# Two fused transformer blocks on one core: the fifth and sixth weight slot run side by side in the start-up, and three smaller edits

## The chip, the cores and the metric

The kernel runs on one core of a Trainium2 chip. The metric is the device time of one execution in microseconds, as a median of runs. An engine works through its own queue in order: TensorE (PE) multiplies matrices, its weight loads are shown as PEld, VectorE is DVE, ScalarE is ACT, SP issues most of the transfers.

## What is computed

Two blocks of two layers each act on x of 512 tokens by 1024 features, batch 1, in fp32. The first block's layer is a modulated RMS norm, an input projection to 28 column tiles of 128, three token mixers (a 31-tap convolution, dilated window attention, and HGRN2, a gated linear scan in both directions), an output projection, and a convolutional FFN. The second block's layer has a top-k sparse attention (A), a sliding-window attention with sinks (B) and stick-breaking attention (C). The two parts that the change touches most, cut:

```python
# modulation and norm, ahead of the input projection
mod = cond @ w_ada[l] + b_ada[l]
sh1, sc1, g1, sh2, sc2, g2 = split(mod, 6)
h = rmsnorm(x, norm1_w[l]) * (1 + sc1) + sh1        # then h @ w_in

# stick-breaking: A[t,s] = beta_ts * prod_{s<j<t}(1 - beta_tj), s < t
z = einsum('bthd,bshd->bhts', qb, k) * dh ** -0.5
log_beta = log_sigmoid(z)
log_1m = where(strict, log_sigmoid(-z), 0.0)
after = cumsum(log_1m, reverse=True) - log_1m
a = where(strict, exp(log_beta + after), 0.0)
```

## The kernel before

Features lie on the 128 partitions, tokens along the free axis. Weights come in *slots*: one slot is one tile of 128 output columns, 8 chunks of 128x128 that multiply the 8 tiles of h (128x512). A product with fp32 accuracy is made of three products of rounded parts: with w = hi + lo and h = hh + hl it is hi·hh, hi·hl, lo·hh (`k_step`, line 811). `w_hi` (746) makes hi with a copy that `copy` (367) gives to ScalarE or VectorE, whichever its clocks say is done first; `w_lo` (764) makes lo = raw - hi on VectorE. `his`, `splits` and `loads` (787, 793, 778) bring the slots up to a number to the state copied, split, loaded. The raw weights have three buffers, so a load waits until the lo of the slot three before is made.

The order of all instructions on each engine is the program's. A planner writes it: streams (attention, scan, convolution) are generators, and `run` (820) and `products` (849) step them between the projection's matmuls whenever the planner's own clocks say that their operands are there. `Timed.charge` keeps these clocks by a cost for each operation.

`start_up` (542) has an order written out by hand. The modulation is a product with `w_ada`, done on VectorE: one row of 128 outputs is one load of 512 KB (`ada`) and one scalar_tensor_tensor with an accumulator over 128x1024 (`mac`). The eight scale rows come first. The first FIRST = 4 slots (`duo`) don't wait for the norm: they multiply x times its scale in plain fp32, tile by tile, as x and the scale rows land (`prep`, `h_raw`); the norm's factor per token (`self.rb`) multiplies their sums afterwards (`scaled`), and the shift's part comes in as a bias, `bias_mm` (961): for each of the eight tiles, one-column products of the four slots' weights with the shift column, eight records of TensorE. The eight shift rows are loaded and multiplied next (`shift`, 593), each a row of 128x1024 and an addition of one column. Then h itself is made for the slots after the fourth: `h_tile` (1148) makes t = x·A1·rb on VectorE, hh = t + B on ScalarE (rounded), and hl = (t + B) - hh on VectorE.

In the kernel before all eight shift rows stand ahead of or among the first two h tiles (lines 612 to 632), all eight bias tiles stand on TensorE ahead of the fifth slot, the splits of slots five to seven are set among the h tiles by WAT, and slot five runs only when `start_up` is over, in `run`, then slot six. `norm_done` adds the bias to the four sums and spawns `hand_on` (997), which gives them to their consumers. `lower_bounds` (692), a dozen small operations and one Exp for the scan's gates, is made during the last start-up tile.

`attend` (1184) serves all attentions: for a tile of 128 queries it makes the scores of two heads on TensorE in a PSUM bank, `score` turns them into weights, `rest` finishes these, then they are transposed and multiplied with V. In `attC_stream` (1894) `score` takes two sigmoids of the scores, of -z and of z; a strict triangular mask is added to the scores on TensorE as a product of a bf16 identity with a bf16 mask (lines 1216 to 1219, `extra`); `rest` scans the first from the right with products and multiplies. `att1_stream` (1326) is the window attention; its `rest` normalises one head on VectorE and one on ScalarE. `scan_stream` (1361) has seven levels; in each, two products of 128x256 update the keys K of both directions (1406 to 1409).

Of the kernel before, what the change touches and what calls it, by code (L numbers as in the profile page):

```python
# [17 lines left out]
P = 128  # L18
S = 512
# [20 lines left out]
RAWAT = (5, 7)  # L40
WAT = [0, 1, 2, 6, 7, 9]
# [153 lines left out]
class Kernel:  # L195
# [297 lines left out]
    def setup(self):  # L493
# [12 lines left out]
        self.hraw = {}  # L506
        self.held_done = 0
# [17 lines left out]
        self.strb = ct("strb", [P, P], BF16)  # L525
        self.idb = ct("idb", [P, P], BF16)
# [15 lines left out]
    def start_up(self):  # L542
# [3 lines left out]
        duo = self.slots[:FIRST]  # L546
# [25 lines left out]
        for n in range(KT):  # L572
            ada(n)
            self.load(self.x[:, n, :], self.i["xT"][:, n, :])
            if n in (0, 2, 3):
                c = slice(*((0, 2 * P), None, (2 * P, 4 * P), (4 * P, KT * P))[n])
                for d in duo:
                    self.load(d.raw[:, c], d.src[:, c])
# [19 lines left out]
        for n in range(KT):  # L598
            if n < KT - 1:
                prep(n + 1)  # L600
            else:
# [7 lines left out]
                lower = self.lower_bounds()  # L609
                next(lower)  # L610
                self.act(self.warm, self.ones[:, 0:1], AF.Sqrt)
                shift(0)
                next(lower, None)
                shift(1)
            for j, (d, p) in enumerate(zip(duo, accs)):
# [26 lines left out]
        self.splits(FIRST + 3)  # L642
        for t in tmps:
            t.free()
# [3 lines left out]
        self.norm_done(duo, ts, bb, True)  # L648

# [25 lines left out]
    def load_consts(self):  # L675
# [12 lines left out]
        self.acopy(self.strb, self.strf)  # L688
        self.acopy(self.idb, self.ident)
# [56 lines left out]
    def w_hi(self, j):  # L746
# [14 lines left out]
        self.copy(s.hi[:, :n], s.raw[:, :n])  # L761
# [422 lines left out]
    def attend(self, heads, span, stride, size, score, V, vo, tag, done, extra=0, groups=((0,), (1,), (2,), (3,))):  # L1184

# [9 lines left out]
        for g in range(len(groups) + 1):  # L1195
            new = []
            for qt in groups[g] if g < len(groups) else ():
                kt0, n = span(qt)
                small = n <= 256
                Ps, tmp = [], []  # L1200
                for bufs, units in ((Ps, 1 if small else 2), (tmp, extra // 2 if small else extra)):
                    for _ in range(units):
                        bufs.append((yield from self.alloc(1)))
                m, x = ([b.ap[:, o:o + n] for b in bufs for o in range(0, U, 256 if small else U)] for bufs in (Ps, tmp))
                new.append((qt, kt0, n, m, x, Ps, tmp))
            if new:
                scs = yield from self.banks("sc")
                at, views = 0, []
                for qt, kt0, n, *_ in new:
                    views.append([sc[:, at:at + n] for sc in scs])  # L1210
                    for hh in range(2):
                        rows = slice(64 * hh, 64 * hh + 64)
                        self.mm(views[-1][hh], q.ap[rows, qt * P:(qt + 1) * P], k.ap[rows, kt0 * P:kt0 * P + n],
                                not (extra and at), not extra, 0.858 * n / S)
# [5 lines left out]
                for (qt, kt0, n, m, x, Ps, tmp), sc in zip(new, views):  # L1220
                    self.did = 0.0
                    rest = score(qt, n, sc, m, *x)
                    made.append((qt, kt0, n // P, m, Ps, tmp, rest, self.did - 0.2))
# [3 lines left out]
            for _ in groups[g - 1] if g else ():  # L1227
                j, kt0, nk, m, Ps, tmp, rest, t = made.pop(0)
# [4 lines left out]
                for x in tmp:  # L1233
                    x.free()
# [91 lines left out]
    def att1_stream(self, p, q, k, vbox, out):  # L1326
# [12 lines left out]
        def score(qt, n, sc, m):  # L1339
# [21 lines left out]
    def scan_stream(self, l, p, q, T0b, Kb, vbox, gbox, out):  # L1361
# [37 lines left out]
        for lev in range(7):  # L1399
# [494 lines left out]
    def attC_stream(self, q, k, vbox, gbox, ys, key, tag):  # L1894
# [15 lines left out]

        def done():
# [3 lines left out]
                                    tag, done, 2, CAUSAL)  # L1915
# [436 lines left out]
```

## Time and profile before

| | |
|---|---|
| median of three runs | 2576.47 us (2575.38 to 2577.38) |
| profiled execution | 2577.97 us |
| its span | 2576.1 us |
| TensorE busy | 98% of the span |
| VectorE busy | 69% |
| ScalarE busy | 52% |
| granted clock, mean | 0.996 |

The profile is one execution. A line of the timeline has the start, the length in us, the engine, the line of the program (L114 and L348 are helpers through which all go, so the tiles' names tell operations apart), the operation, output<-input, shapes, a count where equal instructions are merged, and in brackets how long the engine stood idle before it and what ended that. Matmuls overlap their neighbours, so their pace is read from starts, not from lengths. [...]

### The profile page before, as it was taken

The page shows a single profiled execution, that of the slowest core. Times are in us where ns is not written, and L with a number is a line of the kernel's source. Part 1 is how long each engine was busy: PE and PEld are TensorE (multiplying, and loading weights), DVE is VectorE, ACT ScalarE, POOL GpSimd, SP SyncE. Part 2 cuts the span into 40 slices and gives each one's busy share as a digit, 9 for nine tenths or more (in the row PEclk, how much of TensorE's full clock was granted, in tenths as well). Part 3 has the DMA queues.
Part 4 walks back from the last instruction along what each step waited for, and adds up shares of the span by engine and source line. Part 5 has one row for each costly group of instructions (what it writes and reads, how often), then busy time and mean ns, then how long its engine had stood idle before and what let it go on. Part 6 is the DMA issues. An engine that isn't in the chain of part 4 may idle for free.

```text
span 2576.1 us, 39146 instructions
## 1 busy us (share of the span) xinstructions
PE 2520.9 (98%) x15404; PEld 1991.2 (77%) x15404; DVE 1771.2 (69%) x3364; ACT 1338.2 (52%) x2343; POOL 0.2 (0%) x4
## 2 busy tenths in 40 slices
PE   9999999999999999999999999999999999999998
PEld 5767788888976768888887667777789667777787
DVE  7897777656679768665667985566556895546645
ACT  4686653323357665442336455667435556656622
POOL 0000000000000000000000000000000000000000
PEclk9999999999999999999999999999999999999999
DMA  6433324444333222444342223232332112222222
GB/s 255 140 133 127 123 98 145 147 150 153 116 121 123 98 92 90 139 139 139 131 139 83 75 74 107 93 108 100 110 126 95 66 62 86 91 78 91 86 91 90
DMA packets 90071, 290.32 MB, mean 113 GB/s; under 512 B 10016, under 2 KB 13728, under 8 KB 89888
## 3 DMA queue, kind: packets, MB, share of 16 engines
q1 hardware_dynamic: 87728, 281.76, 32.5%
q10 hardware_dynamic: 2160, 6.06, 0.7%
q8 instruction: 122, 2.00, 0.3%
q14 instruction: 61, 0.50, 0.1%
HBM read 285.69 MB, written 2.10 MB: 112 GB/s over the span
## 4 chain that ended last, share of the span: by engine, by line
PE 77%; DVE 14%; ACT 6%; issue 2%; DMA 2%; SPq 0%; ACTq 0%; DVEq 0%
PE proj L348 65%; DVE arena L114 7%; PE sc L348 6%; ACT arena L114 3%; PE tr L352 3%; PE pva L348 2%; DVE lo L114 2%; DVE sm L114 2%; ACT L114 1%; PE pvs L348 1%; DVE stay L114 1%; PE tr L348 1%; DVE hl L114 1%; DVE ada L114 1%; ACT hi L114 0%
## 5 line engine op out<-in xcount | busy, mean ns | idle before, releaser
L348 PE MATMUL proj<-hh,hi 128*128 128x512 f32 (+1 forms) x2232 | 894.8, 401 | 7.8 <-ACT arena L114 2.7
L348 PE MATMUL proj<-hl,hi 128*128 128x512 f32 (+1 forms) x2232 | 869.1, 389 | 5.9 <-DVE hl L114 5.7
L348 PE MATMUL proj<-hh,lo 128*128 128x512 f32 (+1 forms) x2232 | 869.4, 390 | 0.5 <-DVE lo L114 0.5
L348 PEld LDWEIGHTS proj<-hh,hi 128*128 128x128 f32 x2232 | 420.0, 188 | 133.0 <-issue 36.9
L114 DVE TENSOR_TENSOR lo<-raw,hi 128x1024 fp32r<-128x1024 f32 (+2 forms) x381 | 436.1, 1145 | 94.9 <-ACT hi L114 90.7
L348 PEld LDWEIGHTS proj<-hh,lo 128*128 128x128 f32 x2232 | 419.8, 188 | 90.3 <-DVE lo L114 1.0
L348 PEld LDWEIGHTS proj<-hl,hi 128*128 128x128 f32 x2232 | 420.5, 188 | 86.8 <-DVE hl L114 9.1
L114 ACT CAST hi<-raw 128x1024 fp32r<-128x1024 f32 (+2 forms) x343 | 336.2, 981 | 98.7 <-PE proj L348 63.6
L348 PE MATMUL proj<-rar,hi 128*128 128x512 f32 x672 | 208.8, 392 | 0.0
L114 DVE SCALAR_TENSOR_TENSOR arena<-proj,colt,arena 128x511 f32<-128x511 f32 x164 | 122.9, 749 | 103.8 <-ACT arena L114 100.9
L114 DVE TENSOR_TENSOR arena<-arena 128x512 f32<-128x512 f32 (+10 forms) x316 | 169.7, 557 | 24.6 <-ACT arena L114 17.8
L114 ACT ACT_TABLE_LOAD x132 | 169.4, 1283 | 18.3 <-DVE sm L114 5.7
L114 ACT COPY arena<-tr 128x512 f32<-128x512 f32 (+3 forms) x259 | 109.0, 459 | 119.3 <-PE tr L352 110.1
L114 DVE SCALAR_TENSOR_TENSOR ada<-ada,cbc 128x1024 f32<-128x1024 f32 x128 | 155.8, 1218 | 0.2 <-DMA ada<-ada 0.2
L114 ACT ACTIVATE arena<-proj 128x512 f32<-128x512 f32 x121 | 71.6, 599 | 154.8 <-PE proj L348 152.0
L348 PEld LDWEIGHTS proj<-rar,hi 128*128 128x128 f32 x672 | 124.8, 188 | 28.3 <-issue 3.3
L114 ACT ACTIVATE arena<-proj,colt 128x512 f32<-128x512 f32 x82 | 56.4, 687 | 171.1 <-PE proj L348 169.0
L114 ACT ACTIVATE arena<-arena,sm 128x512 f32<-128x512 f32 (+3 forms) x195 | 114.2, 586 | 53.7 <-DVE sm L114 52.6
L348 PE MATMUL sc<-arena 64*32 64x32 f32 (+6 forms) x3056 | 135.6, 249 | 3.9 <-issue 3.2
L348 PE MATMUL proj<-mx,hi 128*128 128x512 f32 x432 | 136.2, 396 | 2.5 <-DVE x L114 2.5
L352 PE MATMUL tr<-ident,arena 128*128 128x128 f32 x792 | 120.6, 277 | 17.5 <-DVE arena L114 13.1
L114 DVE SCALAR_TENSOR_TENSOR x<-proj,mod,x 128x512 f32<-128x512 f32 (+1 forms) x102 | 64.6, 634 | 104.0 <-PE proj L348 103.1
(220 smaller groups left out, 3068.3 us busy)
## 6 DMA issues: line engine op xcount, KB each, us to landing
raw<-w_in SPq DMA_DIRECT2D x190, 512.0 KB, 3.3
ada<-ada SPq DMA_DIRECT2D x128, 512.0 KB, 4.6
raw<-w_up SPq DMA_DIRECT2D x88, 512.0 KB, 3.3
raw<-w_out SPq DMA_DIRECT2D x32, 512.0 KB, 3.4
raw<-w_down SPq DMA_DIRECT2D x32, 512.0 KB, 3.6
raw<-w_br SPq DMA_DIRECT2D x48, 256.0 KB, 2.7
arena<-ada SPq DMA_DIRECT2D x16, 512.0 KB, 7.3
raw<-w_down SPq DMA_DIRECT2D x16, 384.0 KB, 3.2
```

The lines of the kernel that those rows point to most:

```text
L114: return f(*a, **kw)
L348: self.nc.tensor.matmul(out, lhsT, rhs, start=start, stop=stop)
L352: self.nc.tensor.transpose(out, in_, self.ident)
```

## The change

In `start_up` the fifth and sixth slot (`pair`) run inside, side by side: after the last tile of the first four slots, two h tiles are started, both slots are split (their casts on ScalarE), and then for each tile n: t and hh of tile n+1, hl of tile n, one of the four late shift rows (4 to 7), and the three products of both slots. The seventh slot is split at tile 4. The last four bias tiles stand behind the pair's products, then the two slots are consumed, then the first four sums are scaled. The first four slots' weights are loaded in four quarters, ahead of every other tile; the raw weights of slots five and six move up among the shift rows (RAWAT). `lower_bounds` moves into `hand_on`.

In stick-breaking one sigmoid is left, of -z; the mask on TensorE goes; `rest` sets the diagonal block's masked values to 1 by one scalar_tensor_tensor, scans, takes the difference of neighbours, and sets the last column to zero. The window attention normalises both heads on ScalarE. The scan's two key products become one. Of the diff the parts that only drop arguments (`extra`, `tmp`, `x`) are cut:

```diff
-RAWAT = (5, 7)
-WAT = [0, 1, 2, 6, 7, 9]
+RAWAT = (2, 4)
...
         for n in range(KT):
             ada(n)
             self.load(self.x[:, n, :], self.i["xT"][:, n, :])
-            if n in (0, 2, 3):
-                c = slice(*((0, 2 * P), None, (2 * P, 4 * P), (4 * P, KT * P))[n])
+            if n % 2 == 0:
+                c = slice(n * P, (n + 2) * P)
                 for d in duo:
                     self.load(d.raw[:, c], d.src[:, c])
...
-                lower = self.lower_bounds()
-                next(lower)
                 self.act(self.warm, self.ones[:, 0:1], AF.Sqrt)
                 shift(0)
-                next(lower, None)
                 shift(1)
...
                     if j == 1:
                         self.drain("norm")
-                        self.his(FIRST + 1)
-                    shift(j + 2)
-        tmps = [self.arena.get(1) for _ in range(4)]
-        for n in range(KT + 1):
-            if FIRST + 2 + n < KT:
-                shift(FIRST + 2 + n)
-            if FIRST + n < KT:
-                self.bias_mm(bb, duo, FIRST + n)
-            for k in range(3):
-                if n == WAT[2 * k]:
-                    self.his(FIRST + 1 + k)
-                if n == WAT[2 * k + 1]:
-                    self.splits(FIRST + 1 + k)
-            self.h_tile(n, tmps, KT)
+                    if j < 2:
+                        shift(j + 2)
+
+        ts = [self.arena.get(1) for _ in range(KT)]
+        hs = [(self.hh[:, n, :], self.hl[:, n, :], self.nB[:, n:n + 1]) for n in range(KT)]
+        accs2 = [self.psum("proj") for _ in pair]
+
+        def upper(n):
+            self.stt(ts[n].ap, self.x[:, n, :], self.A1[:, n:n + 1], self.rb.ap, ALU.mult, ALU.mult)
+            self.act(hs[n][0], ts[n].ap, AF.Identity, bias=hs[n][2])
+
+        def lower(n):
+            self.stt(hs[n][1], ts[n].ap, hs[n][2], hs[n][0].bitcast(F32), ALU.add, ALU.subtract)
+            ts[n].free()
+        self.hi_copy = self.acopy
+        upper(0)
+        upper(1)
+        self.splits(FIRST + 2)
+        self.hi_copy = self.copy
+        for n in range(KT):
+            if 0 < n < KT - 1:
+                upper(n + 1)
+            lower(n)
+            if n + 4 < KT:
+                shift(n + 4)
+            for s, p in zip(pair, accs2):
+                self.k_step(s, p, n, n == 0, n == KT - 1)
+            if n == KT // 2:
+                self.loads(FIRST + 2 + self.PD)
+                self.splits(FIRST + 3)
+        for n in range(4, KT):
+            self.bias_mm(bb, duo, n)
+        for s, p in zip(pair, accs2):
+            s.consume(p)
+            self.through(s)
         ts = self.scaled(accs)
...
     def hand_on(self, duo, ts):
+        yield from self.lower_bounds()
...
-                if extra:
-                    for (qt, kt0, n, *_), sc in zip(new, views):
-                        for hh in range(2):
-                            self.mm(sc[hh][:, qt * P:n], self.idb, self.strb, False, qt == groups[g][-1], 0.06)
...
-                self.ts(m[0], m[0], rs[:, 2 * qt:2 * qt + 1], None, ALU.mult)
-                self.act(m[1], m[1], AF.Copy, scale=rs[:, 2 * qt + 1:2 * qt + 2])
+                for hh in range(2):
+                    self.act(m[hh], m[hh], AF.Copy, scale=rs[:, 2 * qt + hh:2 * qt + hh + 1])
...
-            self.v.tensor_mul(sub(K, 0, [[2 * c, n], [1, c]]), sub(K, 0, [[2 * c, n], [1, c]]),
-                              sub(t, Tn + 1, [[2, n], [0, c]]))
-            self.v.tensor_mul(sub(K, S + c, [[2 * c, n], [1, c]]), sub(K, S + c, [[2 * c, n], [1, c]]),
-                              sub(t, 0, [[2, n], [0, c]]))
+            Kd = sub(K, 0, [[S + c, 2], [2 * c, n], [1, c]])
+            self.v.tensor_mul(Kd, Kd, sub(t, Tn + 1, [[-Tn - 1, 2], [2, n], [0, c]]))
...
-        def score(qt, n, sc, m, *gs):
+        def score(qt, n, sc, m):
             for hh in range(2):
-                self.act(gs[hh][:, 0:n], sc[hh][:, 0:n], AF.Sigmoid, scale=-1.0)
-                self.act(m[hh], sc[hh][:, 0:n], AF.Sigmoid)
+                self.act(m[hh], sc[hh][:, 0:n], AF.Sigmoid, scale=-1.0)
...
                 for hh in range(2):
-                    rev = gs[hh][:, 0:n][:, ::-1]
+                    d = m[hh][:, qt * P:n]
+                    self.stt(d, self.strf, -1.0, d, ALU.is_lt, ALU.max)
+                    rev = m[hh][:, ::-1]
                     self.v.tensor_tensor_scan(rev, rev, self.ones[:, 0:1].to_broadcast([P, n]), 1.0,
                                               op0=ALU.mult, op1=ALU.mult)
-                    self.v.tensor_mul(m[hh][:, 0:n - 1], m[hh][:, 0:n - 1], gs[hh][:, 1:n])
+                    self.v.tensor_sub(m[hh][:, 0:n - 1], m[hh][:, 1:n], m[hh][:, 0:n - 1])
+                    self.v.memset(m[hh][:, n - 1:n], 0.0)
```

## Rows read from the trace of the kernel before

**Rows 1.** The page's first part: an engine's busy time, share, instructions.

```profile
PE 2520.9 (98%) x15404; PEld 1991.2 (77%) x15404; DVE 1771.2 (69%) x3364; ACT 1338.2 (52%) x2343; POOL 0.2 (0%) x4
```

**Rows 2.** Timeline of the start-up, VectorE and ScalarE: start, length (us), engine, operation.

```profile
39.84 0.58 ACT L114 COPY arena<-tr 128x512 f32<-128x512 f32 x1 [6.00 <-PE tr L348]
...
40.10 1.22 DVE L114 SCALAR_TENSOR_TENSOR arena<-arena,cbc 128x1024 f32<-128x1024 f32 x1
...
41.44 1.22 DVE L114 SCALAR_TENSOR_TENSOR arena<-arena,cbc 128x1024 f32<-128x1024 f32 x1
...
46.12 1.22 DVE L114 TENSOR_TENSOR lo<-raw,hi 128x1024 fp32r<-128x1024 f32 x1
...
48.03 0.72 ACT L114 ACTIVATE hh<-arena,mod 128x512 fp32r<-128x512 f32 x1 [2.41 <-DVE arena L114]
...
48.66 1.03 ACT L114 CAST hi<-raw 128x1024 fp32r<-128x1024 f32 x1
...
51.23 0.74 DVE L114 SCALAR_TENSOR_TENSOR arena<-x,A,arena 128x512 f32<-128x512 f32 x1
...
51.89 0.74 DVE L114 SCALAR_TENSOR_TENSOR hl<-arena,mod,hh 128x512 fp32r<-128x512 f32 x1
...
58.11 0.75 DVE L114 SCALAR_TENSOR_TENSOR hl<-arena,mod,hh 128x512 fp32r<-128x512 f32 x1 [0.36 <-ACT hh L114]
```

**Rows 3.** The same timeline, TensorE (PE).

```profile
36.06 0.95 PE L348 MATMUL tr<-mod,arena 128*128 128x1 f32 x8
...
36.87 1.10 PE L348 MATMUL sc<-stay,arena 128*128 128x512 f32 x2
...
42.20 7.18 PE L348 MATMUL tr<-mod,arena 128*128 128x1 f32 x40
...
51.10 0.63 PE L348 MATMUL proj<-hl,hi 128*128 128x512 f32 x1
...
51.53 0.63 PE L348 MATMUL proj<-hh,lo 128*128 128x512 f32 x1
...
59.48 0.40 PE L348 MATMUL proj<-hh,hi 128*128 128x512 f32 x1
...
64.95 0.39 PE L348 MATMUL proj<-hh,hi 128*128 128x512 f32 x1
```

**Rows 4.** Instructions that read the tile strb: ns shortest/median/longest, first and last start.

```profile
L348 PE MATMUL sc<-strb,idb x64: 219/219/230, 1390.4 to 2119.0; 128*128 128x128 bf16 x64
```

**Rows 5.** Timeline around the first use of strb, TensorE.

```profile
1390.44 0.40 PE L348 MATMUL sc<-strb,idb 128*128 128x128 bf16 x4
...
1390.65 0.48 PE L348 MATMUL proj<-hh,hi 128*128 128x512 f32 x1
```

**Rows 6.** Windows: length, PE, PEld, DVE, ACT, POOL busy (x), PEclk, DMA, GB/s.

```profile
159.88:163.30 3.42, 1.12 (x5) 0.64 (x4) 3.02 (x5) 3.39 (x5) 0.00 (x0) 0.98 0.43 176
...
163.30:166.70 3.40, 3.40 (x13) 2.56 (x13) 3.09 (x5) 3.40 (x6) 0.00 (x0) 0.52 0.01 2
...
192.00:256.00 64.00, 60.24 (x1108) 44.28 (x1105) 50.24 (x122) 42.32 (x80) 0.00 (x0) 1.00 0.38 131
...
1450.00:1500.00 50.00, 47.10 (x249) 33.70 (x248) 48.29 (x109) 23.26 (x52) 0.00 (x0) 1.00 0.24 80
```

**Rows 7.** Groups of instructions, 60 to 345 us, VectorE: xcount | busy us, mean ns.

```profile
L114 DVE TENSOR_TENSOR arena<-arena 128x512 f32<-128x512 f32 x32 | 21.9, 687 | 4.0 <-ACT arena L114 3.8 <-PE sc L348 0.2
...
L114 DVE TENSOR_TENSOR arena<-arena 128x256 f32<-128x256 f32 x31 | 11.7, 422 | 4.7 <-ACT arena L114 4.7
...
L114 DVE SCALAR_TENSOR_TENSOR stay<-x,A,stay 128x256 f32<-128x256 f32 x16 | 7.6, 483 | 1.6 <-ACT stay L114 1.1
```

**Rows 8.** Timeline at the end of the start-up, ScalarE.

```profile
63.06 1.28 ACT L114 ACT_TABLE_LOAD   x1 [1.84 <-DVE arena L114]
...
64.35 0.64 ACT L114 ACTIVATE arena<-arena 128x512 f32<-128x512 f32 x1
```

**Rows 9.** Groups of instructions, whole span, ScalarE, shapes kept apart.

```profile
L114 ACT ACTIVATE arena<-sc 128x512 f32<-128x512 f32 x44 | 23.5, 604 | 15.2 <-PE sc L348 12.6 <-DVE arena L114 1.4 <-issue 1.2
```

More of the change, by code (lines that the diff above doesn't have):

```diff
@@ L524, in setup @@
         self.strf = ct("strf", [P, P])
-        self.strb = ct("strb", [P, P], BF16)
-        self.idb = ct("idb", [P, P], BF16)
         self.nsink = ct("nsink", [P, 16])
@@ L545, in start_up @@
         b, l = self.cfg[0]
-        duo = self.slots[:FIRST]
+        duo, pair = self.slots[:FIRST], self.slots[FIRST:FIRST + 2]
         self.v.memset(self.sq2, 0.0)
@@ L626, in start_up @@
                         self.drain("norm")
-                        self.his(FIRST + 1)
-                    shift(j + 2)
-        tmps = [self.arena.get(1) for _ in range(4)]
-        for n in range(KT + 1):
-            if FIRST + 2 + n < KT:
-                shift(FIRST + 2 + n)
-            if FIRST + n < KT:
-                self.bias_mm(bb, duo, FIRST + n)
-            for k in range(3):
-                if n == WAT[2 * k]:
-                    self.his(FIRST + 1 + k)
-                if n == WAT[2 * k + 1]:
-                    self.splits(FIRST + 1 + k)
-            self.h_tile(n, tmps, KT)
+                    if j < 2:
[13 more added lines that the diff above has]
+        self.splits(FIRST + 2)
+        self.hi_copy = self.copy
+        for n in range(KT):
[14 more added lines that the diff above has]
+            self.through(s)
         ts = self.scaled(accs)
-        self.splits(FIRST + 3)
-        for t in tmps:
-            t.free()
         for r in (*raws, *self.hraw.values()):
@@ L648, in start_up @@
         self.norm_done(duo, ts, bb, True)
+        self.cur += len(pair)
     def ada_mac(self, w, b, l, t):
@@ L687, in load_consts @@
         mf.free()
-        self.acopy(self.strb, self.strf)
-        self.acopy(self.idb, self.ident)
         self.ts(self.nsink, self.nsink, -1.0, None, ALU.mult)
@@ L760, in w_hi @@
             return False
-        self.copy(s.hi[:, :n], s.raw[:, :n])
+        self.hi_copy(s.hi[:, :n], s.raw[:, :n])
         return True
@@ L1182, in pv_add, with attend @@
                  rhs, start, stop, n)
-    def attend(self, heads, span, stride, size, score, V, vo, tag, done, extra=0, groups=((0,), (1,), (2,), (3,))):
+    def attend(self, heads, span, stride, size, score, V, vo, tag, done, groups=((0,), (1,), (2,), (3,))):
         q, k = heads
@@ L1199, in attend @@
                 small = n <= 256
[L1200 to L1205, printed above, removed]
+                Ps = []
+                for _ in range(1 if small else 2):
+                    Ps.append((yield from self.alloc(1)))
+                m = [b.ap[:, o:o + n] for b in Ps for o in range(0, U, 256 if small else U)]
+                new.append((qt, kt0, n, m, Ps))
             if new:
@@ L1213, in attend @@
                         self.mm(views[-1][hh], q.ap[rows, qt * P:(qt + 1) * P], k.ap[rows, kt0 * P:kt0 * P + n],
-                                not (extra and at), not extra, 0.858 * n / S)
+                                True, True, 0.858 * n / S)
                     at += n
-                if extra:
-                    for (qt, kt0, n, *_), sc in zip(new, views):
-                        for hh in range(2):
-                            self.mm(sc[hh][:, qt * P:n], self.idb, self.strb, False, qt == groups[g][-1], 0.06)
-                for (qt, kt0, n, m, x, Ps, tmp), sc in zip(new, views):
+                for (qt, kt0, n, m, Ps), sc in zip(new, views):
                     self.did = 0.0
-                    rest = score(qt, n, sc, m, *x)
-                    made.append((qt, kt0, n // P, m, Ps, tmp, rest, self.did - 0.2))
+                    rest = score(qt, n, sc, m)
+                    made.append((qt, kt0, n // P, m, Ps, rest, self.did - 0.2))
                 yield (self.clock,)
@@ L1227, in attend @@
             for _ in groups[g - 1] if g else ():
-                j, kt0, nk, m, Ps, tmp, rest, t = made.pop(0)
+                j, kt0, nk, m, Ps, rest, t = made.pop(0)
                 if t > self.clock:
@@ L1232, in attend @@
                 rest()
-                for x in tmp:
-                    x.free()
                 if self.did > self.clock + MARGIN:
@@ L1914, in attC_stream @@
         pv = yield from self.attend((q, k), lambda qt: (0, (qt + 1) * P), 3 * P, 13 * P, score, chunked(vbox[0]), (0, 64),
-                                    tag, done, 2, CAUSAL)
+                                    tag, done, groups=CAUSAL)
         vbox[0].free()
```

## The prediction

> **What bounds the kernel now.** I read the page's busy times first, then the timeline of the first 65 us, then windows over the stages that hold the other edits. TensorE is busy 2520.9 us of the 2576.1 us span [rows 1]: only 55 us are idle, and a third of the span's worth of VectorE time is free on average. So a change is worth what it takes from TensorE's own instructions, or from the few places where TensorE stands still. VectorE work saved elsewhere is hidden.
>
> In the start-up the reader is to see a different order of limits. The four plain-fp32 slots keep TensorE in a row until about 43 us; the broadcast of the norm lands on ScalarE at 39.84+0.58 = 40.42 [rows 2]. Only then can VectorE make h, and from there VectorE is the limit until its last hl, at 58.11+0.75 = 58.86 [rows 2]. TensorE has the fifth slot ready almost at once after that: the sixth starts at 59.48, the seventh at 64.95, that is 24 matmuls in 5.47 us, 0.228 us each [rows 3]. Before them, at 42.20, stand 40 bias records, 7.18 us long [rows 3]; they lie in time in which h was not there yet, so they cost next to nothing. I measure the start-up by the seventh slot's first matmul: 64.95 us.
>
> **Start-up, step by step.** Nothing up to about 43 us moves on TensorE: the same 32 products, norm and first four bias tiles, in the same order. The weights of the first four slots come in quarters, the last behind the seventh scale tile; the bytes ahead of the eighth are the same, and I price this at nothing: TensorE needs the last quarter about two tiles later than it lands. If that cover failed it would cost a load. The fifth and sixth raw weights move ahead of three shift tiles each on SP's queue, so those tiles land later, by one or two loads; the late ones are used only after 46 us, long after. The lower-bound arithmetic leaves VectorE here (about 2 us, in time in which VectorE then has nothing to do before 40.42) and comes back behind the start-up.
>
> From 40.42: VectorE makes t0 and t1, one per 0.66 us (51.23 to 51.89 [rows 2]), t1 done at 41.85. ScalarE makes hh0, hh1 (0.72 each [rows 2]), done at 42.6, and only then casts the fifth weights (1.03 [rows 2]), done at 43.6, and the sixth, 44.6. VectorE waits 1.8 us for the first cast, since the two weight subtractions stand next in its queue. They take 1.22 each [rows 2], to 46.0; then hl0, 46.65. TensorE's second product of the pair waits for that. From then on each tile costs VectorE t, hl (0.66 each) and one late shift row, 1.34 us (40.10 to 41.44 [rows 2]): 2.66 us. So hl1, hl2, hl3 and hl4 come at 49.35, 52.0, 54.7 and 57.35 us. At tile 4 the seventh slot's cast stands on ScalarE behind hh5: VectorE waits some 1.1 us for it and subtracts 1.13 to 1.22 us; hl5 comes at 61.0, hl6 at 62.3, hl7 at 62.95. TensorE has 6 products per tile, 1.37 us at 0.228: five remain after hl5 (62.1), twelve more follow, 64.85. Then the four last bias tiles, now behind the pair: 32 records, 0.81 us per eight (36.06 to 36.87 [rows 3]), 3.25 us. The seventh slot starts at 68.1 instead of 64.95: **+3.2 us**. What is queued behind the waits is named: behind VectorE's wait for the cast stand all hl; behind TensorE's wait for hl stand the bias tiles, and behind these the scaling of the first four results.
>
> [...] So the start-up is between +3.2 and +4.9; I take **+4.0**, in the middle, since the fall depends on where the hole lies.
>
> **Stick-breaking.** 64 masking products leave TensorE [rows 4]. Four of them take 1390.44 to 1390.65, 0.053 us each [rows 5]: 64 x 0.053 = **-3.4 us**, on the path, because TensorE is the limit there. 64 sigmoids of at most 0.60 us leave ScalarE [rows 9], which is not the limit. VectorE gets 64 scalar_tensor_tensor over 128 columns and 64 one-column memsets more; the product becomes a subtraction of equal size. The nearest row for the first is 0.483 us at 256 columns [rows 7]; half of it to the whole of it bounds one at 0.24 to 0.48, I take 0.3, so 19 us over two layers, and a few for the memsets. I cost them at nothing, hidden behind projections; the cover is thin where VectorE is busy 48.29 of 50 us [rows 6], which is a rival below.
>
> **Scan and window attention.** The merged product takes 0.687 instead of 2 x 0.422 us [rows 7]: 0.157 x 42 = 6.6 us of VectorE. 24 normalisations go from VectorE to ScalarE, at most 0.72 us each there [rows 2]: 17 us of ScalarE over two layers. Both hidden: 0. All orders are laid out anew by the planner, since its clocks start from another state. So the chance stall at 160 us, 3.42-1.12 = 2.3 us of idle plus 1.7 us of low clock [rows 6], need not come back; I take half of its 4.0 us, **-2.0**, bounds 0 and -4.0.
>
> The lower bounds' Exp stands now between two Sigmoids instead of between Square and Sqrt: one table load more. A load at 63.06 let the next activation start at 64.35 [rows 8], so 1.29 us, off TensorE's path. [...]
>
> **Sum.** The profiled execution took 2577.97 us (span 2576.1 and 1.9 around it), 1.5 above the median of the three runs, 2576.47. 2577.97 + 4.0 - 3.4 - 2.0 = 2576.6; less 1.5, about **2575.0 us** as a median.
>
> **Rivals.** [...] (2) *Slower: VectorE in the stick-breaking stretch.* At 1450 to 1500 us VectorE is busy 48.29 and TensorE idle 2.9 of 50 us [rows 6], waiting for scans. If half of the 20 added us shows up as TensorE waits, +10: 2585. It decides once TensorE waits over 0.11 us more at each of the 32 query tiles, which is what two masks of 0.053 us give back. Against it: the top-k rounds there can yield. (3) *Faster: the relief of VectorE in the first two layers.* At 192 to 256 us TensorE is idle 3.8 of 64 us [rows 6]. If the 6.6 and some 10 us taken from VectorE, with the new order, remove about as much in each of the four such stretches of two layers, half of 16 us, -8 (of it 2 in the forecast): 2569. It speaks against it that ScalarE gets more. (4) *The change doesn't do what it says*: the pair gains no head start, because hl0 comes two microseconds later than 46.65; all behind it moves by as much, +6 in place of +4: 2577.
>
> **How the numbers follow.** Forecast 0.37; (1) 0.12, (2) 0.13, (3) 0.33, (4) 0.05. A measurement of this kernel can tell about 0.2%, 5.2 us, from no change: faster is below 2571.3, slower above 2581.6. (3) is faster; the forecast and (4) are same; (1) is half same, half slower; (2) is slower, with 0.03 of the forecast. Faster 0.34, same 0.45, slower 0.21. The forecast's own range is 2572 to 2579, from its bounds (+3.2 to +4.9; 0 to -4.0). The 8-in-10 range reaches from (3) to nearly (2): 2566 to 2584.
>
> **What would show it.** First product of the pair with hl near 46.7 us, one tile per 2.66 us, hl7 near 63, 32 bias records behind it, the seventh slot's first product near 68 (PEclk low once). No masking products; TensorE's waits for transpositions in the two stick-breaking stretches as before. No 2 us hole at 160. It would be wrong if VectorE did the shift rows while it waited for the casts, if those bias tiles found a gap, or if the new order opened a hole elsewhere.

## The result, and the profile after

The changed kernel takes 2590.34 us (median of four runs, 2588.15 to 2593.04) beside 2576.43 us for the kernel before on the same chip: ratio 1.0054, 95% interval 1.0042 to 1.0067. It is **13.9 us slower**; 2575.0 was forecast, and 2584 was the upper end of the range. The profiled execution took 2589.65 us, with a span of 2587.9: 11.8 us more than the span before.

The page's first part of the changed kernel, an engine's busy time, share and instructions:

```profile
PE 2520.5 (97%) x15340; PEld 1990.5 (77%) x15340; DVE 1791.7 (69%) x3446; ACT 1301.2 (50%) x2267; POOL 0.2 (0%) x4
```

Beside [rows 1]: 64 products fewer, VectorE 20.5 us more, ScalarE 37 us less, all as the change says. TensorE's busy time fell by 0.4 us only, so it stood still 12.2 us longer; the time that a lower clock adds hides in the busy time (below, 5 us hold 23 records of TensorE at the full clock and 14 at 0.57 of it, busy 5.00 us in both), where 64 products left it. Where? The projections' 9168 products stand in the same order in every kernel here (but for the pair, whose two slots alternate in the new start-up). So the start of a product in one trace, less the start of the same product in the trace before, is the delay at that point. Worked out so, at four points (times of the kernel before):

| | 75 us | 363 us | 1337 us | 2565 us (the last product) |
|---|---|---|---|---|
| changed kernel | +6.7 | +1.9 | +3.8 | +11.2 |

Up to 75 us is the start-up, up to 363 us layer 1's mixers, up to 1337 us all the rest of the first block, and from there the second block, where the only stick-breaking is. The end adds 0.6. Each delay comes from one execution. The ten changed kernels below that keep the old start-up lie between -1.0 and +1.4 us at 75 us, so a tenth means nothing, three microseconds do.

**The start-up.** TensorE's timeline of the changed kernel; columns as in [rows 3]:

```profile
46.53 0.80 PE L347 MATMUL proj<-hl,hi 128*128 128x512 f32 x1 [2.30 <-DVE hl L113]
...
60.80 0.50 PE L347 MATMUL proj<-hl,hi 128*128 128x512 f32 x1 [1.96 <-DVE hl L113]
...
64.80 4.42 PE L347 MATMUL tr<-mod,arena 128*128 128x1 f32 x32
69.08 0.77 PE L347 MATMUL proj<-hh,hi 128*128 128x512 f32 x1
69.65 0.63 PE L347 MATMUL proj<-hl,hi 128*128 128x512 f32 x1
...
74.32 0.40 PE L347 MATMUL proj<-hh,hi 128*128 128x512 f32 x1
```

The pair's first hl product at 46.53, its end at 64.80, the seventh slot's first product at 69.08 instead of 64.95 [rows 3]: +4.1 us. Then that slot's products come 0.43 us apart until 74.32, where 0.228 was the pace before. The windows say why; first the changed kernel, 65 to 70 and 70 to 75 us (length, busy PE, PEld, DVE, ACT, POOL, then PEclk, the clock that TensorE was granted as a share of the full one, DMA, GB/s):

```profile
65.00:70.00 5.00, 5.00 (x33) 4.89 (x33) 2.93 (x5) 4.93 (x5) 0.00 (x0) 0.74 0.02 3
70.00:75.00 5.00, 5.00 (x14) 3.86 (x13) 4.81 (x13) 0.20 (x2) 0.00 (x0) 0.57 0.16 45
```

and the run after_scanprice (below), whose operations stand in the same order up to 1400 us (PE alone, then PEclk, DMA, GB/s):

```profile
65.00:70.00 5.00, 5.00 (x40) 1.00 0.01 3
70.00:75.00 5.00, 5.00 (x23) 1.00 0.15 32
```

with its timeline at the bias records:

```profile
64.86 3.63 PE L349 MATMUL tr<-mod,arena 128*128 128x1 f32 x32
68.35 0.48 PE L349 MATMUL proj<-hh,hi 128*128 128x512 f32 x1
```

The same order ran from 70 to 75 us at 0.57 of the clock in one execution and at 1.00 in the other. At full clock (PEclk 1.00 from 64.60 to 68.40 us in after_scanprice) the 32 one-column products take 3.49 us and the seventh slot comes at 68.35, +3.4 us; the delay at 75 us is +3.5. In the profiled execution of the changed kernel they take 4.28 (0.81 from 64.80 to 69.08), and the slot behind them runs at the lower clock (0.57 from 70 to 75): +4.1 and +6.7. So the start-up itself costs what was forecast, and the clock adds some 3 us in this execution. The eight kernels here that have this start-up, with the bias tiles behind the pair, lie between +3.5 and +8.5 us at 75 us. What decides is not shown; from 44 to 51 us the two executions had already had different clocks, 0.55 and 0.76.

**The second block.** TensorE's waits, grouped by what ended them (us in total, times, longest), for the transpositions of the attentions, in the kernel before and in the changed one:

```profile
PE tr L352 <- DVE arena L114: 13.1, 24, 1.1
```

```profile
PE tr L351 <- DVE arena L113: 22.0, 26, 3.5
```

That is 8.9 us more. One such wait from close by, the changed kernel's timeline for a query tile with 384 keys (other work left out):

```profile
2062.28 0.28 DVE L113 SCALAR_TENSOR_TENSOR arena<-strf,arena 128x128 f32<-128x128 f32 x1
...
2062.60 0.96 DVE L113 TENSOR_TENSOR_SCAN arena<-arena,ones 128x384 f32<-128x384 f32 x1
...
2063.59 0.56 DVE L113 TENSOR_TENSOR arena<-arena 128x383 f32<-128x383 f32 x1
...
2064.19 0.29 DVE L113 SCALAR_TENSOR_TENSOR arena<-strf,arena 128x128 f32<-128x128 f32 x1
...
2064.30 0.52 PE L351 MATMUL tr<-ident,arena 128*128 128x128 f32 x3
...
2064.51 0.96 DVE L113 TENSOR_TENSOR_SCAN arena<-arena,ones 128x384 f32<-128x384 f32 x1
...
2065.51 0.56 DVE L113 TENSOR_TENSOR arena<-arena 128x383 f32<-128x383 f32 x1
...
2066.13 0.06 DVE L113 MEMSET arena<- 128x1 f32 x1
...
2066.21 0.52 PE L351 MATMUL tr<-ident,arena 128*128 128x128 f32 x3 [1.39 <-DVE arena L113]
```

The first head is transposed at 2064.30. The second head's mask, scan, difference and memset run from 2064.19 to 2066.19, and TensorE stands 1.39 us with that transposition at the head of its queue. The planner believed in less: `charge` prices a scan at 0.067 + 0.00104 us a column, 0.47 for 384. The trace has 0.96. All sizes, grouped:

```profile
L113 DVE TENSOR_TENSOR_SCAN arena<-arena,ones 128x512 f32<-128x512 f32 x16 | 19.6, 1224 | 0.6
L113 DVE SCALAR_TENSOR_TENSOR arena<-strf,arena 128x128 f32<-128x128 f32 x64 | 18.2, 285 | 1.4
...
L113 DVE TENSOR_TENSOR_SCAN arena<-arena,ones 128x128 f32<-128x128 f32 x16 | 6.8, 425 | 0.6
```

From 425 to 1224 ns over 384 columns is 2.08 ns each, twice the slope of an ordinary product, (687-422)/256 = 1.04 [rows 7]. The kernel before has the same wrong price, with a chain shorter by mask and memset.

### The profile page after: what moved, and what is told of

It reads as the page before. It is cut to its first block, busy times and chain, and to the rows that moved or that the text cites. A ratio compares the mean times of both kernels' runs of the same rounds, so it can differ in the third digit from the quotient of the medians.

```text
span 2587.9 us, 38979 instructions
## 1 busy us (share of the span) xinstructions
PE 2520.5 (97%) x15340; PEld 1990.5 (77%) x15340; DVE 1791.7 (69%) x3446; ACT 1301.2 (50%) x2267; POOL 0.2 (0%) x4
## 4 chain that ended last, share of the span: by engine, by line
PE 80%; DVE 13%; ACT 5%; issue 2%; DMA 0%; DVEq 0%; ACTq 0%; SPq 0%
PE proj L347 66%; DVE arena L113 8%; PE sc L347 6%; PE pva L347 3%; ACT arena L113 3%; PE tr L351 3%; DVE lo L113 2%; PE pvs L347 2%; DVE sm L113 1%; PE tr L347 1%; ACT L113 1%; DVE ada L113 1%; DVE hl L113 0%; ACT stay L113 0%; ACT hi L113 0%
## 5 line engine op out<-in xcount | busy, mean ns | idle before, releaser
L113 ACT CAST hi<-raw 128x1024 fp32r<-128x1024 f32 (+2 forms) x336 | 329.6, 982 | 99.5 <-PE proj L347 65.3
L113 DVE TENSOR_TENSOR arena<-arena 128x512 f32<-128x512 f32 (+10 forms) x294 | 170.6, 596 | 26.6 <-ACT arena L113 21.1
L113 ACT ACTIVATE arena<-arena,sm 128x512 f32<-128x512 f32 (+2 forms) x213 | 125.5, 601 | 79.1 <-DVE sm L113 77.8
L113 ACT COPY arena<-tr 128x512 f32<-128x512 f32 (+3 forms) x249 | 103.8, 454 | 116.2 <-PE tr L351 107.9
L113 ACT ACT_TABLE_LOAD x118 | 151.4, 1283 | 19.2 <-DVE sm L113 11.2
L347 PE MATMUL sc<-arena 64*32 64x32 f32 (+5 forms) x3024 | 138.3, 253 | 1.2 <-issue 1.1
L351 PEld LDWEIGHTS tr<-ident,arena 128*128 128x128 f32 x775 | 92.4, 141 | 57.6 <-issue 15.6
```

The source lines that it names most:

```text
L113: return f(*a, **kw)
L347: self.nc.tensor.matmul(out, lhsT, rhs, start=start, stop=stop)
L351: self.nc.tensor.transpose(out, in_, self.ident)
```

## The experiments

The theory after this reading, **A**: the loss is a sum of the parts, start-up +3.5 to +6.7 and stick-breaking +7 to +10, the rest nothing. Its rival, **B**: every edit makes the planner lay out another order, and that moves the time more than the edits do. For stick-breaking itself, **V** (VectorE has too little time) stood against **P** (the planner's price of the scan puts the transpositions too early). All medians are device us, the ratio against the kernel before, run beside it.

**Each part alone, and no part.** The new start-up alone:

> The kernel before with the new start-up alone (pair of slots by tiles of h, late shift rows, lower bounds after it); stick-breaking, normalisation and scan keys stay as before. Theory A (the sum of the parts): the seventh slot's first matmul comes at about 69.1 us instead of 64.95, the granted clock is 0.5 from about 67.4 to 74.3 us, and by 75 us the delay is +6.6 us; layer 1's mixers give some 2 us back, so the whole is +3 to +6 us (2579 to 2583). Theory B (the order that is planned anew moves the time more than the parts do): any sign; the stall of 4.4 us near 921 us stands here as well, and the whole is outside +3 to +6.

Measured: 2590.96 (ratio 1.0053, 1.0040 to 1.0065). Delay +8.5 at 75 us, **+16.3 at 363 us**, +15.2 at the end. The stick-breaking alone:

> The kernel before with the one-sigmoid stick-breaking alone. Theory A: 4 fewer mask products' worth of TensorE time (-3.4 us over the span), but TensorE's waits for VectorE before transpositions grow by about 9 us, most of it in the second block's stick-breaking and half a microsecond per query tile of 512 keys: +4 to +9 us (2581 to 2585). Theory B: the waits of the stick-breaking stretch stay within 3 us of those before and the time moves by stalls elsewhere, of either sign.

Measured: 2598.43 (1.0083, 1.0069 to 1.0097). Delay 0.0 at 75 us, **+11.2 at 363 us**, +10.1 at 1337, +20.0 at the end. The normalisation and the keys, without the other two:

> The kernel before with the first attention's normalisation on ScalarE for both heads and the scan keys in one instruction per level, nothing else. Theory A: both lie beside TensorE, 0 within 1.5 us (2575 to 2578). A rival, that the stall at 921 us of the changed kernel belongs to the normalisation on ScalarE: a stall of 3 to 5 us with two table loads beside it appears near 915 us here, and the time is +4 to +8 us with the low clock behind it.

Measured: 2579.01 (1.0007, 0.9999 to 1.0016): same, though a stall of 4.2 us near 921 us stands in it, as the rival said. And the kernel before with

```diff
     def charge(self, name, op, a, kw):
+        self.nch = getattr(self, 'nch', 0) + 1
+        if self.nch % 400 == 0:
+            self.t[name] += 1.0
```

> The kernel before, with no operation changed: only the planner's own clock of VectorE or ScalarE is moved on by 1 us at every 400th operation that it prices (about ten times in all), so that the order is planned anew. Theory A: within 1.5 us of the kernel before. Theory B: the order alone moves the time by 3 us or more, with stalls of over 2 us at places that the kernel before does not have.

Measured: 2575.97 (0.9998, 0.9989 to 1.0007). The whole is as A expected, though +2.7 at 363 us and 4.8 back afterwards; B's new stalls of over 2 us did not come.

The two large parts alone lose 13.7 and 21.1 us, all together 13.9. A sum of parts they are not. But in the second block, from 1337 us on, A holds within 4 us: start_alone -0.4, norm_keys_alone +1.9, stick_alone +9.9, the changed kernel +7.4. Layer 1 is where it breaks down: stick_alone loses 11.2 us in a layer that has no stick-breaking at all. Its timeline there (ScalarE, VectorE, TensorE; other work left out):

```profile
263.12 0.60 PE L352 MATMUL tr<-ident,arena 128*128 128x128 f32 x4
...
265.43 0.30 ACT L114 ACTIVATE sm<-sm,eps 128x4 f32<-128x4 f32 x1 [2.47 <-DVE sm L114]
265.74 1.28 ACT L114 ACT_TABLE_LOAD   x1
...
267.04 0.60 ACT L114 ACTIVATE arena<-proj 128x512 f32<-128x512 f32 x1
267.67 0.69 DVE L114 TENSOR_TENSOR arena<-proj,arena 128x512 f32<-128x512 f32 x1 [0.31 <-ACT arena L114]
268.27 0.74 DVE L114 SCALAR_TENSOR_TENSOR arena<-arena,colt,tr 128x512 f32<-128x512 f32 x1
269.05 0.69 DVE L114 TENSOR_TENSOR arena<-arena 128x512 f32<-128x512 f32 x1
269.16 1.09 PE L352 MATMUL tr<-ident,arena 128*128 128x128 f32 x4 [5.44 <-DVE arena L114]
```

TensorE stands 5.44 us before one transposition. That waits for VectorE, which waits for the activation at 267.04, which stands on ScalarE behind a square root and a table load; ScalarE had itself stood 2.47 us for a result of VectorE (sm). (That load lets the next activation start 1.30 us after its own start, 265.74 to 267.04.) In start_alone the same place holds TensorE for 7.5 us.

**Is it the order?**

> The new start-up alone, as in start_alone, with the planner's clock of VectorE or ScalarE moved on by 1 us at every 400th operation that it prices (as in nudge); no operation is changed. Theory B (the 10 us that start_alone loses between 212 and 305 us are an accident of the order, a transposition queued on TensorE behind table loads on ScalarE): the 7.7 us stall near 272 us is not there, and the time is 2580 to 2583, the +4 to +6.6 us of the start-up itself. Theory A' (the later start of the fifth to eighth slots makes that stall, whatever the order): it stands again, and the time is 2588 to 2593.

Measured: 2596.83 (1.0077, 1.0062 to 1.0092), delay 4.9 at 75 us and 22.4 at 363. My expectation for B was wrong, and the time lies above that for A' as well: in place of one stall of 7.5 us there are three, of 5.0, 3.0 and 2.5. So this other order doesn't free the new start-up of its loss in layer 1, but the size of that loss isn't fixed either.

**What of stick-breaking costs?** One sigmoid with the mask left on TensorE:

```diff
-                for bufs, units in ((Ps, 1 if small else 2), (tmp, extra // 2 if small else extra)):
+                for bufs, units in ((Ps, 1 if small else 2), (tmp, 0)):
...
-                self.act(gs[hh][:, 0:n], sc[hh][:, 0:n], AF.Sigmoid, scale=-1.0)
-                self.act(m[hh], sc[hh][:, 0:n], AF.Sigmoid)
+                self.act(m[hh], sc[hh][:, 0:n], AF.Sigmoid, scale=-1.0)
```

with the difference in `rest` as in the change.

> The kernel before with one sigmoid, scan, difference and last column cleared, but the mask still added on TensorE as before, so that VectorE has no 128x128 mask operation. From 1337 us on, where the second block's mixers lie, stick_alone loses 9.8 us. Theory V (the mask operation of 0.285 us in front of each scan makes the transpositions wait): the loss from there falls to 0 to 3 us. Rival (the difference in place of the product, or the order): 7 us or more stay. For layer 1 before that no number is expected, since its order is planned anew.

Measured: 2580.70 (1.0015, 1.0005 to 1.0024); +4.6 from 1337 us on. Between the two: about half of the loss of 9.9 is the mask on VectorE, half stays without it. Layer 1 gave -1.0 from 75 to 363 us. Then the price:

```diff
         elif op == "reciprocal":
             c = 0.07 + n * 0.0064
+        elif op == "tensor_tensor_scan":
+            c = 0.152 + n * 0.00208
```

> The one-sigmoid stick-breaking alone, with one change to the planner: it prices the scan along a row at 0.152 + 0.00208 us per element, as the trace has it (0.42 us for 128, 1.22 us for 512), instead of 0.067 + 0.00104. Theory P (the transposition of the second head is placed too early because the chain of mask, scan and difference takes some 1.2 us longer for two heads than it is priced): TensorE's waits of 1.2 to 1.6 us before transpositions from 1400 us on go, and the loss from 1337 us on falls from 9.8 us to 0 to 4. Theory V (VectorE has too little time in that stretch, whatever the order): 7 us or more stay, as waits at other products.

Measured: 2576.47 (0.9998, 0.9989 to 1.0007): 22 us faster than stick_alone, **-12.1 instead of +9.9** from 1337 us on, and +10.1 at 363 us, nearly as in stick_alone.

> The kernel before with the scan priced as the trace has it and nothing else. Theory P: TensorE's waits for VectorE before transpositions in the second block (1.0 to 1.25 us each) go, -2 to -5 us (2571 to 2575). Theory V: within 1.5 us of before.

Measured: **2561.48** (0.9936, 0.9920 to 0.9953). Three times the most that I expected. TensorE's idle time (span less busy time) fell from 55.2 to 43.1 us; its busy time fell by 3.7 with the same products, and why stays open. Its waits for the transpositions, and its window in the stick-breaking stretch (columns as above):

```profile
PE tr L354 <- DVE arena L114: 1.6, 2, 1.3
```

```profile
1450.00:1500.00 50.00, 50.00 (x266) 37.22 (x265) 45.62 (x96) 27.05 (x60) 0.00 (x0) 1.00 0.26 90
```

and the same window of the changed kernel:

```profile
1450.00:1500.00 50.00, 45.64 (x235) 32.63 (x234) 47.89 (x114) 20.96 (x41) 0.00 (x0) 1.00 0.21 74
```

Before, VectorE was busy 48.29 of these 50 us and TensorE 47.10 [rows 6]. With the price right, TensorE is busy all 50. P holds, and V falls as the main cause: VectorE was full, but it didn't bind; the transposition stood too early.

> The kernel before with one sigmoid, the mask still on TensorE, and the scan priced as the trace has it. Theory P: in layer 1 as without that price (-2.0 us at 363 us), and the second block within 3 us of the kernel before with that price (-15 us from 1337 us on): 2558 to 2562. Rival (the longer chain on VectorE still counts): 2563 to 2568.

Measured: 2563.77 (0.9946, 0.9933 to 0.9960), -10.5 from 1337 us on. That is the rival's range: the one-sigmoid form still costs 4.7 us beside before_scanprice, even with the mask on TensorE.

**All four edits with that price, and without some.**

> The changed kernel, with the scan priced to the planner as the trace has it. Theory P: up to 1337 us it runs as the changed kernel (+1.9 us to before at 363 us, +3.8 at 1337), and from there on it gains some 12 us where the changed kernel loses 7, as the one-sigmoid stick-breaking did with this price: 2566 to 2571. Rival: the gain is eaten by other waits in the second block, 2575 to 2580.

Measured: 2567.23 (0.9962, 0.9949 to 0.9976); -13.4 from 1337 us on, waits for the transpositions 5.4 us instead of 22.0, as P expected. Four forms have now run with both prices, and from 1337 us on the true price gives 15.2, 22.0, 15.1 and 20.8 us (before, stick_alone, stick_pemask, the changed kernel): that is no luck of one order. So 23 us of the changed kernel hang on one price of the planner. Without normalisation and keys:

> The same without the normalisation on ScalarE and without the merged scan keys: new start-up, one-sigmoid stick-breaking and the true price of the scan. Either of the two edits alone lost 10 us and more between 212 and 305 us, the changed kernel with all four lost 0.3 there. Theory N (the work that the normalisation and the keys take from VectorE is what keeps that stretch free): the stall of 5 to 8 us near 270 us stands, the delay at 363 us is +10 us or more, the time 2576 to 2585. Rival (which order comes out is an accident): at 363 us between -2 and +5, the time 2564 to 2572.

Measured: 2578.08 (0.9999, 0.9990 to 1.0009); +12.8 at 363 us, with the 7.5 us stall near 269 us again, as theory N expected. Which of the two edits takes it away?

> New start-up, one-sigmoid stick-breaking and normalisation on ScalarE, without the merged scan keys; the scan priced as the trace has it. If the normalisation is what takes away the stall near 270 us: the delay at 363 us is -1 to +5 us and the time 2564 to 2571, with the stall of 4.4 us near 921 us if that is its price. If it is the keys: +10 us or more at 363 us, 2576 or more.

> New start-up, one-sigmoid stick-breaking and merged scan keys, without the normalisation on ScalarE; the scan priced as the trace has it. The other way round: if the keys take the stall near 270 us away, -1 to +5 us at 363 us; if the normalisation does, +10 us or more at 363 us, no stall near 921 us, and the time is 2575 or more.

Measured: 2571.43 (0.9976, 0.9967 to 0.9986) and 2567.66 (0.9963, 0.9948 to 0.9977), with +2.9 and +4.7 at 363 us. Either does it alone, so neither is the one cause. The stall of the changed kernel near 921 us,

```profile
923.45 1.28 ACT L113 ACT_TABLE_LOAD   x1
924.74 0.60 ACT L113 ACTIVATE arena<-proj 128x512 f32<-128x512 f32 x1
...
925.37 0.69 DVE L113 TENSOR_TENSOR arena<-proj,arena 128x512 f32<-128x512 f32 x1 [4.04 <-ACT arena L113]
...
926.12 1.22 PE L347 MATMUL proj<-mx,hi 128*128 128x512 f32 x2 [4.22 <-DVE arena L113]
```

is of the same kind (an activation behind a table load). It stands, 4.2 us long, in norm_keys_alone, after_scanprice and start_norm_keys (below) too; in start_stick_norm it is 1.8 us, in start_stick_keys it is gone, and so it is in stick_norm_keys (next), which has both edits. It isn't the normalisation's own price.

> All but the new start-up, the scan priced as the trace has it. The changed kernel with that price takes 2567; the start-up's own +3.5 us (its delay at 75 us there) goes, if nothing gives it back: 2562 to 2565, and the delay at 363 us is -4 to -1 us. If layer 1 gives the start-up back (its order absorbs a later start): 2566 to 2569. If the stall near 270 us comes back without it: 2575 or more.

Measured: 2561.39 (0.9938, 0.9923 to 0.9952), -5.2 at 363 us, both a little below what was expected. Without the new start-up the rest is 5.8 us faster than with it.

> All but the one-sigmoid stick-breaking, the scan priced as the trace has it. If normalisation and keys take the stall away that the new start-up alone has: +1 to +5 us at 363 us and 2563 to 2569. If the stall stands: +10 us or more at 363 us, 2573 or more.

Measured: 2566.27 (0.9959, 0.9944 to 0.9974), +0.3 at 363 us, -15.4 from 1337 us on. The time is as expected.

**The bias tiles in the pair's waits.**

```diff
                 self.k_step(s, p, n, n == 0, n == KT - 1)
+            if n in range(1, 5):
+                self.bias_mm(bb, duo, n + 3)
...
-        for n in range(4, KT):
-            self.bias_mm(bb, duo, n)
```

> The changed kernel with the last four bias tiles (32 one-column products, 4.4 us behind the pair) placed between the pair's tiles, where TensorE waits about 2 to 2.8 us for each tile of hl. Theory A: they lie in those waits, the seventh slot's first matmul comes at 64.8 us within 0.5 instead of 69.1, and as those products were what went before the fall of the granted clock at 67.4 us, it stays at 1.0; at 75 us the delay is 0 within 1 us instead of +6.6. Rival: the clock falls all the same after the pair, and the delay at 75 us is +2 to +4. The order of layer 1 is planned anew, so for the whole time no number is expected.

Measured: 2595.45 (1.0072, 1.0058 to 1.0085). The seventh slot's first product came at 65.76 instead of 69.08, 3.3 us earlier, and PEclk was 1.00 from 65 to 75 us. But its timeline goes on (VectorE, TensorE):

```profile
72.69 2.35 DVE L113 TENSOR_TENSOR lo<-raw,hi 128x1024 fp32r<-128x1024 f32 x2
...
73.97 0.50 PE L347 MATMUL proj<-hh,lo 128*128 128x512 f32 x1 [2.01 <-DVE lo L113]
```

The eighth slot's lo is not there: VectorE makes it behind the sums of the first four slots, and TensorE, now earlier, waits 2 us. At 75 us the delay is +3.3; the order of layer 1 then cost +3.7 more. So the clock stayed up, as A said, but the gain that A expected (0 within 1 us at 75 us) went into another wait, and the first product came 0.5 us later than its range.

**Why does stick-breaking lose in layer 1?** ScalarE's timeline of the kernel before shows the only work of layer 1 that this edit takes away:

```profile
69.73 0.30 ACT L114 CAST strb<-strf 128x128 bf16<-128x128 f32 x1
69.93 0.30 ACT L114 CAST idb<-ident 128x128 bf16<-128x128 f32 x1
```

They were put back, with nobody to read them:

```diff
+        self.acopy(self.strb, self.strf)
+        self.acopy(self.idb, self.ident)
```

> The one-sigmoid stick-breaking alone, as in stick_alone, but the two casts (mask and identity to bf16, 0.3 us each on ScalarE near 70 us) put back, though nothing reads them. Theory B (by their absence the order of layer 1 is planned anew, and that order is what stalls near 264 us): the delay at 363 us is -2 to +0.5 us, as in the kernel before, instead of +11.2, the loss from 1337 us on stays +7 to +11, and the whole is 2582 to 2588 instead of 2598. Rival (the freed scratch and ScalarE's other work of the edit matter): +8 us or more at 363 us.

Measured: 2586.10 (1.0036, 1.0022 to 1.0050). **-0.2 at 363 us instead of +11.2**, and +8.9 from 1337 us on. On all engines the operations stand again in the order of the kernel before, up to the first stick-breaking. Two casts of 0.3 us, hidden on ScalarE, decide about 11 us. The windows from 262 to 285 us, stick_alone and then this kernel (columns as above):

```profile
262.00:285.00 23.00, 12.49 (x49) 7.94 (x51) 13.34 (x34) 16.14 (x26) 0.00 (x0) 0.63 0.13 46
```

```profile
262.00:285.00 23.00, 21.90 (x138) 16.73 (x134) 15.29 (x34) 18.35 (x31) 0.00 (x0) 1.00 0.23 82
```

TensorE is busy 12.49 us at 0.63 of the clock against 21.90 at 1.00: the stall, and behind it a lower clock (in stick_alone the four transpositions at 269.16 took 1.09 us, the four at 263.12 ahead of the stall 0.60). For what stick_alone loses in layer 1, B is shown. Last, the two gains together: normalisation, keys and the true price, stick-breaking as before, and the casts moved to the change of phase behind the first block, so that the order of stick_norm_keys comes back in layer 1:

> The kernel before with the normalisation on ScalarE, the merged scan keys, the scan's true price, and the two casts moved behind the last product of the first block; stick-breaking as before. Theory B: up to 1337 us as stick_norm_keys (-5 us), from there as the kernel before with that price (-10 to -15 us): 2556 to 2561. Rival: the two gains don't add, 2562 to 2566.

Measured: **2555.66** (0.9917, 0.9903 to 0.9930), -6.0 at 363 us, -15.5 from 1337 us on, each a little beyond what was expected. It beats both kernels, by 21.6 and some 35 us.

The second block by groups, from 1337 us on: with the product form and the old price 0 (before), -0.4, -4.1, -4.1 and +1.9, mean -1.3; with one sigmoid and the mask on VectorE +7.4, +9.9, +10.9 and +8.9, mean +9.3; with the true price -15.2, -15.4 and -15.5 against -9.8 to -13.4, mean -11.9. So the one-sigmoid form costs about 10.6 us as planned, and 3.5 us with the scan priced rightly.

Layer 1, from 75 to 363 us, over the nineteen kernels here: from -5.3 to +17.5 us.

## Why the prediction was wrong, step by step

- **Start-up, +4.0** (bounds +3.2 to +4.9): +4.1 at the point where it was to be measured. First hl product 46.65 forecast, 46.53; one tile per 2.66 us, as forecast; end of the pair 64.85, 64.80. At full clock the 32 bias records took 3.49 us where 3.25 were forecast, so the lower bound was the undisturbed case (+3.4). The upper bound's 1.7 us were my estimate, half of the 3.40 us at 0.52 of the clock [rows 6], for a fall of the clock in the pair's hole before hl5; the changed kernel does not show it there. In it the low clock came behind the pair, among the bias records and in the slot after them: 0.7 us up to the seventh slot and 2.6 after it. In start_alone it did come in the pair (PEclk 0.82 from 58 to 65 us, products 0.43 us apart up to 65.50, the bias records at 66.58 instead of 64.80), and its seventh slot came +5.9 us late, at 70.82, above the upper bound. What makes the clock fall is not shown: PEclk was 1.00 from 51 to 65 us in the changed kernel in spite of the holes (TensorE busy 9.54 of 14 us), and from 70 to 75 us it was 0.57 and 1.00 for one and the same order. Rival (1), low clock through the whole pair, did not happen, nor did rival (4).
- **Stick-breaking, -3.4, the rest hidden: the step that failed.** The amounts were right: 64 masks of 0.285 us, 18.2 us, where 19 were forecast. "I cost them at nothing, hidden behind projections" was wrong. They are in front of a transposition whose place on TensorE's queue is fixed by the planner, and the second block came out at +7.4 us net in place of -3.4. The mask is about half of it: with the mask back on TensorE the form alone still lost 4.6 us there. The planner's price is the larger part of the loss, not all of it: with the scan priced rightly the form still costs 3.5 us beside the product form, where 3.4 were to be gained. Rival (2) had the place and nearly the size (+10), at a chance of 0.13; its reason, that VectorE is the limit there, fell in the main with before_scanprice.
- **Scan and window attention, 0.** Alone +1.7 us, within the noise. But in the changed kernel they keep layer 1 free of the stall that the other two edits bring there.
- **The chance stall at 160 us, -2.0 (0 to -4.0).** It is gone, and layer 1 gave back 4.8 us after 75 us. The step was sized as if a new order could only remove a stall; its bounds held no loss. The runs show it open on that side: up to +17.5 us in layer 1. Rival (3), 8 us from the relief of VectorE in the first block, did not come: from 75 to 1337 us the changed kernel gave back 2.9.
- **Table load, 0.** As forecast, off the path at the start: the changed kernel's loads at 68.83 and 77.85 us took 1.28 us each, and TensorE was busy 15.00 of 15 us from 65 to 80. What I had not weighed is a table load that a new order puts ahead of an activation for which a transposition waits (1.30 us of the 5.44 in stick_alone).

So the forecast of the median missed by 15 us, of which about 11 are the stick-breaking term (+7.4 instead of -3.4). In the profiled execution the 4.8 us that layer 1 gave back and the 1.9 lost between 363 and 1337 us nearly fit the -2.0 given to new orders; the rest is the clock's 2.6 us, 0.6 at the end, and the scatter of executions (2588 to 2593).

What stays open: why either the normalisation or the keys takes the stall near 270 us away (relief of VectorE, or just another order), why half of the one-sigmoid loss stays with the mask on TensorE, what makes the new start-up alone lose 7.8 us in layer 1 (no run put the old order back under it), and what decides whether the clock falls at 67 us.

## What to carry to other kernels

Where a planner writes the order, first compare its prices with the trace's durations: one wrong price (0.6 for 1.22 us) was worth 15 us, while none of the edits gained anything by itself at the old price. Judge an edit in such a kernel by stretch, from the delay of the same instruction in both traces, and put back the order elsewhere before you compare: two hidden casts of 0.3 us moved the total by 11 us. Work that is hidden on average is not hidden if it lies in a chain ahead of an instruction at the head of an in-order queue, as at 2066.21, where TensorE stood 1.39 us.

## What the runs showed of the hardware

In the changed kernel a scan along a row took 425 ns over 128 columns and 1224 over 512 on VectorE, 2.08 ns per column, twice the 1.04 of an ordinary product of two tiles (422 ns over 256 columns, 687 over 512 [rows 7]).

Whether TensorE's clock fell among 32 one-column products differed between two executions of the same order: over the products PEclk was 1.00 in after_scanprice and 0.81 in the changed kernel, and from 70 to 75 us 1.00 and 0.57, at 5.00 of 5 us busy in both.
